# Two stacked transformer blocks on one core: when weights are split at the end of a projection, which engine computes three modulation vectors, and which one squares x in the opening

## The chip, the cores and the metric

The kernel runs on one core of a Trainium2 chip. The core has TensorE (PE; its weight loads are PEld), VectorE (DVE), ScalarE (ACT), GpSimd (POOL) and SyncE (SP, which here only issues transfers). Each engine works through its own instructions in the order in which they were written for it; semaphores make one wait for another. The metric is the device time of one execution in microseconds (us).

## The reference

Input `x` has 256 positions of 1024 numbers. Two blocks of two layers each follow each other. A layer is a mixer and a feed-forward part, each behind a modulated norm; the modulation comes from a condition vector `c`:

```python
def first_block(x, c, positions, ...):
    cond = jax.nn.silu(c)
    for l in range(DEPTH):                      # DEPTH = 2
        mod = cond @ w_mod[l] + b_mod[l]        # six vectors of 1024
        sh1, sc1, gt1, sh2, sc2, gt2 = [m[:, None, :] for m in jnp.split(mod, N_MOD, axis=-1)]
        h = rms_norm(x, norm_g[l, 0]) * (1.0 + sc1) + sh1
        y = mixer_block(h, positions, w_in[l], ...)   # conv, NSA, GLA, gMLP, then @ w_o
        x = x + gt1 * rms_norm(y, norm_g[l, 1])
        h = rms_norm(x, norm_g[l, 2]) * (1.0 + sc2) + sh2
        y = jnp.square(jax.nn.relu(h @ w_up[l])) @ w_down[l]
        x = x + gt2 * rms_norm(y, norm_g[l, 3])
    return x

def second_block(x, c, ...):
    c_act = jax.nn.silu(c)
    for l in range(DEPTH):
        mod = (c_act @ ada_w[l] + ada_b[l])[:, None, :]
        sh_m, sc_m, gt_m, sh_f, sc_f, gt_f = jnp.split(mod, 6, axis=-1)
        h = rms_norm_2(x, norm_mix[l]) * (1 + sc_m) + sh_m
        y = hybrid_mixer(h, ...) if l % 2 == 0 else retention_mixer(h, ...)
        x = x + gt_m * y
        h = rms_norm_2(x, norm_ffn[l]) * (1 + sc_f) + sh_f
        x = x + gt_f * swiglu(h, ffn_w_in[l], ffn_w_out[l])
    return x
```

All weights are float32, and the result is to be accurate as in float32.

## The kernel before, in words

**Data.** `x` stays on the chip, transposed: eight chunks of 128 features by 256 positions. A matrix is read in loads `w` of 1 MB (128 x 2048, pool of `W_BUFS` = 4), issued on SP in program order. `load_split` cuts a load into two halves of 128 x 1024 and each into a high part `wh` (a cast on ACT, L214) and the rest `wl` (a subtraction on DVE, L217). The activations are split alike: `hh` on ACT (L211), `hl` on DVE (L233), after `h` on DVE (L233). A product is then three matmuls (`hh` by `wh`, `hh` by `wl`, `hl` by `wh`) into PSUM tiles `pa`.

**Stages and tails.** The program runs layer by layer: input projection, mixer, output projection, feed-forward up, down. A *tail* is the end of a projection with the norm behind it. In block 1, `post1` sums squares of `y` (`sq`), of the gated tile `t`, and `xt` = t times x over the tiles; `px` matmuls with a matrix of ones sum them over the partitions; `rstd`, three `u` steps, `sx`, `r` follow, and then per chunk an update of `x`, `h`, `hh`, `hl`. In block 2, `post2` adds each tile to `x`, sums its squares, and `rstd` of that sum leads to `h` at once. There are seven tails: the first layer's output projection, three more in block 1, three in block 2 (behind the last projection there is none).

**The hold.** `sums` notes the last Square in `self.tail`. When `post1` or `post2` has read its last tile, it sets `self.tailed = 3`; the casts of the next three loads are then held until that Square has been issued on ACT:

```python
            with self.after(self.tail) if self.tailed else nullcontext():
                self.copy(h[:, :m], w[:, a * n:b * n])
```

`after` sets an order for the scheduler on an engine; where it holds nothing back, the scheduler places instructions by its own estimate of the times.

**Modulation.** `MODE` says how each of the six vectors of a layer is computed. "j": the first two of the first layer, in the opening (`mods_first`). "p": on TensorE (`mod`): eight transfers `mw` of 512 KB, for each four matmuls `pm`, then a copy `row` on ACT and four small transfers `ab<-row` by POOL. "d": on DVE (`mod_rows`): eight transfers, each multiplied by the condition's rows and summed in one instruction (L398, here called a product); `settle` keeps the last ones back until `last_wl`, the split issued last, has been written. The pool `mw` has four buffers. Modulation has a low priority (`LATER`). In the first layer `weave` gives out its steps between those of the mixer at the pace `FILL`; later ones are given out by `carry` at a rate per load.

**Opening.** Constants, angles and squares of the first `x` run in a written order on ACT, eight Squares there; sixteen `px` matmuls and the copy `sx` lead to `r`.

Of the kernel before, what the change touches and what calls it, by code (L numbers as in the profile page):

```python
# [12 lines left out]
AF = mybir.ActivationFunctionType  # L13
# [3 lines left out]
D = 1024  # L17
# [87 lines left out]
CONSTANTS_AT = 3  # L105
EARLY_AT = (0, 2)
AHEAD = 3
SQ_ACT = (0,)
# [3 lines left out]

MODE = {(1, 0): "jjpppd", (1, 1): "dddddd", (2, 0): "dddddd", (2, 1): "dddddd"}

# [8 lines left out]
LOADS = {"ffn10": (32, 3, 4), "ffn11": (32, 3, 4), "ffn20": (38, 3, 4), "ret": (32, 3, 4)}  # L123
FILL = (0.7, 0, 0)
W_BUFS, MW_BUFS, HL_BUFS = 4, 4, 4
# [9 lines left out]
class Prog:  # L135
    def __init__(self, ctx, tc, t):
# [17 lines left out]
        self.plan = None  # L154
        self.pend, self.hold, self.last_wl, self.tail, self.tailed = [], None, None, None, 0

# [160 lines left out]
    def load_split(self, ap, nk, n):  # L317

        w = self.load(ap, nk * n)
        self.tailed = max(self.tailed - 1, 0)  # L320
        parts = []
        hk = (nk + 1) // 2
        for a, b in ((0, hk), (hk, nk)):
            h = self.hlp.tile([128, 1024], F32R, name=self.nm("wh"), tag="wh")
            l = self.hlp.tile([128, 1024], F32R, name=self.nm("wl"), tag="wl")
            m = (b - a) * n
            with self.after(self.tail) if self.tailed else nullcontext():
                self.copy(h[:, :m], w[:, a * n:b * n])
# [56 lines left out]
    def silu_c(self, c):  # L385
        s = self.V(KD)
        self.sigmoid(s, c)
        self.mul(c, c, s)
        rep = self.C(KD, 32)
        self.copy(rep, c[:, :, None].to_broadcast([128, KD, 32]))  # L390
        return rep
# [47 lines left out]
    def mods_first(self, v):  # L439
# [7 lines left out]
        b1 = self.V(KD, s="b1")  # L447
        self.stt(b1, b[:, 8:16], 1.0, g[:, 0:8], ALU.add, ALU.mult)
        quad = self.C(1, s="quad")
# [50 lines left out]
    def sums(self, parts, src, keep=2):  # L500

        q = self.U(S, s="sq")
        self.tail = self.act(q, src, AF.Square)
        self.running(parts, q, keep)
# [21 lines left out]
    def norm_mod(self, r, scale, shift):  # L526

        hs, hm = [], []
        for c in range(4):
# [3 lines left out]
            for j in range(2):  # L533
# [3 lines left out]
                hm.append(self.stt(h[:, j], self.x[:, k], scale[:, k:k + 1], r, ALU.mult, ALU.mult))  # L537
                self.act(hi[:, j], h[:, j], AF.Identity, bias=shift[:, k:k + 1])
                self.last_lo = self.stt(lo[:, j], h[:, j], shift[:, k:k + 1], hi[:, j].bitcast(F32), ALU.add,
                                        ALU.subtract)  # L540
                hs.append((hi[:, j], lo[:, j]))
        self.update = None
        return hs

# [21 lines left out]
    def start(self):  # L566
# [14 lines left out]
        return c  # L581

    def constants(self):
        nc = self.nc
# [7 lines left out]
    def rope_tables(self):  # L592
# [17 lines left out]
        lim = 3.1415925  # L610
        self.ts(a, a, lim, ALU.min, -lim, ALU.max)
        self.act(self.rc, a, AF.Sin)
# [35 lines left out]
    def block1_vecs(self, l):  # L648
# [7 lines left out]
        return v  # L656

    def cond1(self):
        self.rows[1] = self.silu_rows(self.rows_c(self.t["c1"]))
        yield 1  # L660

# [456 lines left out]
    def post1(self, tiles, b, sx, **where):  # L1118
# [3 lines left out]
        for group in tiles:  # L1122
# [7 lines left out]
            for j, y in group:  # L1130
# [3 lines left out]
                self.running(xt, q, keep)  # L1134
        self.tailed = 3
        r = self.rstd(yy, D)
# [437 lines left out]
    def post2(self, tiles, gt, end=False):  # L1574
# [10 lines left out]
        if end:  # L1585
            return None
        self.tailed = 3
        return self.rstd(sq, D)
# [43 lines left out]
    def run(self):  # L1632
# [4 lines left out]
        with self.tc.manual_schedule(engines={mybir.EngineType.Activation}):  # L1637
            self.nc.scalar.preload_act_table_set("natural_log_exp_and_others")
            self.crep = {1: self.silu_c(c)}
            self.rope_tables()  # L1640
            self.nc.scalar.preload_act_table_set("natural_log_exp_and_others")
            sq = []
            for j in range(KD):
                self.sums(sq, self.x[:, j], KD)
            p = self.psum_of(sq)
            sx = self.U(S, s="sx")
            self.copy(sx, p)
            r = self.U(S, s="r2")
            self.rsqrt(r, sx, 1.0 / D)
        self.mods_first(self.v1[0])  # L1650
        for l in range(2):
            if l == 0:
                self.v1.append(self.block1_vecs(1))
                self.v1[1]["norm2"] = self.v1[1]["norm"][:, 16:24]
                self.queue = [self.cond1()] + [self.mods(*a, self.v1[0]) for a in STAGE["mix10"]]
            else:
                self.start2()
# [123 lines left out]
```

## Time and profile before

| what | value |
|---|---|
| three runs, median (lowest to highest) | 1537.33 us (1529.53 to 1538.15) |
| the profiled execution | 1532.73 us |
| its span | 1530.9 us |
| mean granted clock of TensorE | 0.973 |
| TensorE busy | 1445.3 us (94%) |
| VectorE busy | 1139.9 us (74%) |
| ScalarE busy | 808.4 us (53%) |
| moved by DMA | 333.15 MB, 218 GB/s |

Times in the rows are from the start of the span. The profiled execution took 1.8 us more than its span. "Busy" counts an engine's instructions; an idle engine off the chain costs nothing. A granted clock of 1.00 is 2.4 GHz, and half of it 1.2 GHz; a value between is a mean over a stretch.

### The profile page before, as it was taken

To read this page: it belongs to the slowest core of one execution; us is meant where nothing else is said; L and a number is where in the kernel's file an instruction comes from. 1 tells how busy PE (TensorE), PEld (TensorE's weight loads), DVE (VectorE), ACT (ScalarE), POOL (GpSimd) and SP (SyncE) were. 2 spreads that over 40 slices of the span, in tenths; PEclk is the share of its full clock that TensorE was granted. 3 is DMA by queue.
4 is the path that set the end of the run, shared out by engine and by line. 5 is a ranking of instruction groups with operands and counts; after the bars stand their busy time and mean duration, and the time that the engine had idled before them with its cause. 6 is when DMAs were issued, how large, how long until landed. Compare 5 with 4: busy or idle time off the path is not lost.

```text
span 1530.9 us, 28353 instructions
## 1 busy us (share of the span) xinstructions
PE 1445.3 (94%) x11594; PEld 1377.5 (90%) x11594; DVE 1139.9 (74%) x1966; ACT 808.4 (53%) x1348; POOL 19.4 (1%) x57
## 2 busy tenths in 40 slices
PE   7999799998999799998999988999989999899999
PEld 5986699997987799997998778999989999899999
DVE  4774779886786899987887547788678888577664
ACT  5654466544555555443774246565445555466642
POOL 1000100000000000000000000000000000000000
PEclk9999899999999999998999898999999999999999
DMA  9846679994441479983532016666766776445453
GB/s 367 289 189 233 234 258 349 358 336 167 140 188 56 168 286 356 375 316 132 220 113 109 1 56 234 243 233 234 267 246 244 259 257 240 163 157 189 167 168 107
DMA packets 65783, 333.15 MB, mean 218 GB/s; under 512 B 8146, under 2 KB 9460, under 8 KB 41716
## 3 DMA queue, kind: packets, MB, share of 16 engines
q1 hardware_dynamic: 65268, 331.30, 59.2%
q8 instruction: 91, 1.49, 0.4%
q14 instruction: 40, 0.33, 0.1%
q0 software_dynamic: 384, 0.03, 0.0%
HBM read 330.22 MB, written 1.05 MB: 216 GB/s over the span
## 4 chain that ended last, share of the span: by engine, by line
PE 91%; DVE 4%; ACT 2%; DMA 1%; issue 1%; SPq 0%; POOL 0%; DVEq 0%; ACTq 0%
PE pa L236 79%; PE py L236 5%; PE px L236 4%; DVE wl L217 2%; PE po L236 1%; PE pm L236 1%; ACT wh L214 1%; ACT u L211 0%; DMA ab<-row 0%; PE py L239 0%; DVE h L233 0%; DMA mw<-in_wmod 0%; DMA vec<-in_vec 0%; DVE u L217 0%; DVE t L217 0%
## 5 line engine op out<-in xcount | busy, mean ns | idle before, releaser
L217 DVE TENSOR_TENSOR wl<-w,wh 128x1024 fp32r<-128x1024 f32 (+4 forms) x444 | 512.5, 1161 | 214.6 <-ACT wh L214 213.5
L214 ACT CAST wh<-w 128x1024 fp32r<-128x1024 f32 (+4 forms) x444 | 439.9, 999 | 363.8 <-PE pa L236 338.6
L236 PE MATMUL pa<-hh,wh 128*128 128x256 f32 x1920 | 515.6, 289 | 43.9 <-ACT hh L211 43.9
L236 PE MATMUL pa<-hh,wl 128*128 128x256 f32 x1920 | 511.1, 287 | 0.0
L236 PEld LDWEIGHTS pa<-hh,wh 128*128 128x128 f32 x1920 | 373.0, 194 | 51.6 <-ACT hh L211 46.8
L236 PE MATMUL pa<-hl,wh 128*128 128x256 f32 x1920 | 390.1, 285 | 0.0
L236 PEld LDWEIGHTS pa<-hh,wl 128*128 128x128 f32 x1920 | 373.4, 195 | 2.3 <-issue 2.1
L236 PE MATMUL pa<-oh,wh 128*128 128x256 f32 x1184 | 334.4, 286 | 7.4 <-ACT oh L214 7.4
L236 PE MATMUL pa<-oh,wl 128*128 128x256 f32 x1184 | 332.6, 284 | 0.0
L236 PE MATMUL pa<-ol,wh 128*128 128x256 f32 x1184 | 318.6, 283 | 0.2
L236 PEld LDWEIGHTS pa<-hl,wh 128*128 128x128 f32 x1920 | 301.5, 193 | 1.9 <-issue 1.6
L236 PEld LDWEIGHTS pa<-oh,wh 128*128 128x128 f32 x1184 | 227.7, 192 | 12.3 <-ACT oh L214 9.1
L236 PEld LDWEIGHTS pa<-oh,wl 128*128 128x128 f32 x1184 | 226.9, 192 | 2.6 <-issue 1.3
L236 PEld LDWEIGHTS pa<-ol,wh 128*128 128x128 f32 x1184 | 219.2, 191 | 0.6 <-DVE ol L217 0.6
L398 DVE SCALAR_TENSOR_TENSOR mw<-mw,cond 128x1024 f32<-128x1024 f32 x152 | 182.8, 1219 | 0.0
L236 PE MATMUL pa<-wh,hh 128*128 128x256 f32 (+2 forms) x224 | 66.9, 301 | 6.2 <-ACT hh L211 6.2
L236 PE MATMUL pa<-wh,hl 128*128 128x256 f32 (+2 forms) x224 | 66.1, 302 | 1.2 <-DVE hl L233 1.2
L236 PE MATMUL pa<-wl,hh 128*128 128x256 f32 (+2 forms) x224 | 67.1, 300 | 0.0
L211 ACT ACTIVATE sw<-sw 128x256 f32<-128x256 f32 x132 | 55.0, 417 | 3.7 <-DVE sw L230 1.0
L211 ACT ACTIVATE u<-u 128x512 f32<-128x512 f32 (+3 forms) x78 | 42.6, 555 | 18.6 <-DVE u L230 13.1
L211 ACT ACTIVATE hh<-h,mods 128x256 fp32r<-128x256 f32 x64 | 30.7, 505 | 38.8 <-DVE h L233 33.6
L236 PEld LDWEIGHTS pa<-wh,hh 128*128 128x128 f32 x224 | 43.8, 196 | 7.7 <-ACT hh L211 6.6
(359 smaller groups left out, 1348.0 us busy)
## 6 DMA issues: line engine op xcount, KB each, us to landing
mw<-in_wmod SPq DMA_DIRECT2D x176, 512.0 KB, 5.7
w<-in_fwin SPq DMA_DIRECT2D x44, 1024.0 KB, 4.8
w<-in_wup SPq DMA_DIRECT2D x32, 1024.0 KB, 5.0
w<-in_wdn SPq DMA_DIRECT2D x32, 1024.0 KB, 6.7
w<-in_rwin SPq DMA_DIRECT2D x24, 1024.0 KB, 5.0
w<-in_fwo SPq DMA_DIRECT2D x32, 704.0 KB, 4.1
w<-in_win SPq DMA_DIRECT2D x16, 1024.0 KB, 6.1
w<-in_hwin SPq DMA_DIRECT2D x12, 1024.0 KB, 4.8
```

Of the source, the lines that this page charges most:

```text
L211: return self.nc.scalar.activation(out=out, in_=in_, func=func, **kw)
L214: return self.nc.scalar.copy(out, in_)
L217: return (e or self.nc.vector).tensor_tensor(out=out, in0=a, in1=b, op=op)
L236: return self.nc.tensor.matmul(out, lhsT=lhsT, rhs=rhs, start=start, stop=stop, skip_group_check=True)
L398: self.nc.vector.scalar_tensor_tensor(out=w, in0=w, scalar=1.0, in1=cond, op0=ALU.mult, op1=ALU.mult, accum_out=m[:, j:j + 1])
```

## The change

Three things change.

1. The hold on the casts of the three loads behind a tail goes. In its place the *second* `load_split` behind a norm has its casts after the `hh` of chunk 2 of that norm.
2. The first layer's vectors 3 to 5 (indices 2, 3 and 4) are computed as products on DVE ("d"), not by matmuls ("p"). Their pace `FILL` is 1.0, not 0.7. The condition's rows, which DVE needs for that, are loaded and computed in the opening instead of the mixer.
3. In the opening five of the eight squares of `x` go to DVE, 24 matmuls of ones by ones are added on TensorE ahead of the `px` sums, `r` is computed straight from PSUM and `sx` copied behind it, and the table load on ACT stands behind the Squares.

```diff
+X_ACT = (1, 3, 5)
+WARM = 24
-MODE = {(1, 0): "jjpppd", (1, 1): "dddddd", (2, 0): "dddddd", (2, 1): "dddddd"}
+MODE = {(1, 0): "jjdddd", (1, 1): "dddddd", (2, 0): "dddddd", (2, 1): "dddddd"}
-FILL = (0.7, 0, 0)
+FILL = (1.0, 0, 0)
...
     def load_split(self, ap, nk, n):
         w = self.load(ap, nk * n)
-        self.tailed = max(self.tailed - 1, 0)
+        self.since += 1
...
-            with self.after(self.tail) if self.tailed else nullcontext():
+            with self.after(self.hold_act) if self.since == 2 and self.loads > 2 else nullcontext():
                 self.copy(h[:, :m], w[:, a * n:b * n])
...
-        self.stt(b1, b[:, 8:16], 1.0, g[:, 0:8], ALU.add, ALU.mult)
+        with self.after(self.angles):
+            self.stt(b1, b[:, 8:16], 1.0, g[:, 0:8], ALU.add, ALU.mult)
...
-        self.tail = self.act(q, src, AF.Square)
+        self.act(q, src, AF.Square)
...
-                self.act(hi[:, j], h[:, j], AF.Identity, bias=shift[:, k:k + 1])
+                hh = self.act(hi[:, j], h[:, j], AF.Identity, bias=shift[:, k:k + 1])
+                if k == 2:
+                    self.hold_act = hh
...
         self.update = None
+        self.since = 0
         return hs
...
+    def warm(self):
+
+        ps = self.M(128)
+        for i in range(WARM):
+            self.mm(ps, self.ones, self.ones, i == 0, i == WARM - 1)
...
-    def cond1(self):
-        self.rows[1] = self.silu_rows(self.rows_c(self.t["c1"]))
-        yield 1
...
-        self.tailed = 3
         r = self.rstd(yy, D)
...
-        self.tailed = 3
         return self.rstd(sq, D)
...
             self.rope_tables()
-            self.nc.scalar.preload_act_table_set("natural_log_exp_and_others")
             sq = []
             for j in range(KD):
-                self.sums(sq, self.x[:, j], KD)
+                if j in X_ACT:
+                    self.sums(sq, self.x[:, j], KD)
+                else:
+                    q = self.U(S, s="sq")
+                    with self.after(self.angles), self.after(self.silu):
+                        self.mul(q, self.x[:, j], self.x[:, j])
+                    self.running(sq, q, KD)
+            self.nc.scalar.preload_act_table_set("natural_log_exp_and_others")
+            self.warm()
             p = self.psum_of(sq)
+            r = self.U(S, s="r2")
+            self.rsqrt(r, p, 1.0 / D)
             sx = self.U(S, s="sx")
             self.copy(sx, p)
-            r = self.U(S, s="r2")
-            self.rsqrt(r, sx, 1.0 / D)
         self.mods_first(self.v1[0])
+        with self.later(LATER):
+            self.rows[1] = self.silu_rows(self.rows_c(self.t["c1"]))
...
-                self.queue = [self.cond1()] + [self.mods(*a, self.v1[0]) for a in STAGE["mix10"]]
+                self.queue = [self.mods(*a, self.v1[0]) for a in STAGE["mix10"]]
```

What the scheduler makes of it is seen at three places. The first is ACT at the last tail, from the retention's output projection to the second SwiGLU. Before (`sq` of the last tile, casts of the first two loads, `rstd`, `hh` of the norm):

```order
L211 ACTIVATE sq_15076<-x_88 128x256
L214 CAST wh_15124<-w_15122 128x1024
L214 CAST wh_15128<-w_15122 128x1024
L214 CAST wh_15189<-w_15187 128x1024
L214 CAST wh_15193<-w_15187 128x1024
L211 ACTIVATE rstd_15082<-px_15079,eps_90 128x256
L211 ACTIVATE rstd_15082<-rstd_15082 128x256
L211 ACTIVATE hh_15086<-h_15085,mods_11419 128x256 x2
L211 ACTIVATE hh_15095<-h_15094,mods_11419 128x256 x2
```

The same place with the change:

```order
L216 CAST wh_15101<-w_15099 128x1024
L216 CAST wh_15105<-w_15099 128x1024
L213 ACTIVATE sq_14990<-x_88 128x256
L213 ACTIVATE sq_15053<-x_88 128x256
L213 ACTIVATE rstd_15059<-px_15056,eps_90 128x256
L213 ACTIVATE rstd_15059<-rstd_15059 128x256
L213 ACTIVATE hh_15063<-h_15062,mods_11396 128x256 x2
L213 ACTIVATE hh_15072<-h_15071,mods_11396 128x256
L216 CAST wh_15166<-w_15164 128x1024
L216 CAST wh_15170<-w_15164 128x1024
L213 ACTIVATE hh_15072<-h_15071,mods_11396 128x256
```

The first load's two casts moved ahead of the last two Squares, and the second load's between the third and the fourth `hh`.

The second place is DVE at the first tail, behind the first layer's output projection. Before (`xt` of the last tile, splits of the first two loads of the feed-forward part, the `u` steps):

```order
L217 TENSOR_TENSOR xt_1940<-t_1933,x_88 128x256
L217 TENSOR_TENSOR xt_1946<-t_1935,x_88 128x256
L217 TENSOR_TENSOR wl_2113<-w_2110,wh_2112 128x1024
L217 TENSOR_TENSOR wl_2117<-w_2110,wh_2116 128x1024
L217 TENSOR_TENSOR wl_2183<-w_2180,wh_2182 128x1024
L217 TENSOR_TENSOR wl_2187<-w_2180,wh_2186 128x1024
L217 TENSOR_TENSOR u_1964<-rstd_1953,px_1956 128x256
L233 SCALAR_TENSOR_TENSOR u_1964<-px_1960,u_1964 128x256
L217 TENSOR_TENSOR u_1964<-u_1964,rstd_1953 128x256
L217 TENSOR_TENSOR sx_1968<-u_1964,sx_148 128x256
```

The same place with the change (`mw` by `cond` is a product):

```order
L400 SCALAR_TENSOR_TENSOR mw_2015,mod_2006<-mw_2015,cond_433 128x1024
L219 TENSOR_TENSOR u_1976<-rstd_1965,px_1968 128x256
L400 SCALAR_TENSOR_TENSOR mw_2018,mod_2006<-mw_2018,cond_433 128x1024
L235 SCALAR_TENSOR_TENSOR u_1976<-px_1972,u_1976 128x256
L400 SCALAR_TENSOR_TENSOR mw_2021,mod_2006<-mw_2021,cond_433 128x1024
L219 TENSOR_TENSOR u_1976<-u_1976,rstd_1965 128x256
L400 SCALAR_TENSOR_TENSOR mw_2024,mod_2006<-mw_2024,cond_433 128x1024
L219 TENSOR_TENSOR sx_1980<-u_1976,sx_176 128x256
```

The splits left this place, and products stand between the steps of the tail.

The third place is SP's queue at the same tail, from the end of the first layer's output projection (`in_wo`) to the feed-forward part (`in_wup`). Before:

```order
L277 DMA w_1868<-in_wo 128x2048
L277 DMA w_2110<-in_wup 128x2048
L482 DMA mw_1616<-in_wmod 128x1024
L482 DMA mw_1620<-in_wmod 128x1024
L482 DMA mw_1974<-in_wmod 128x1024
L482 DMA mw_1978<-in_wmod 128x1024
L277 DMA w_2180<-in_wup 128x2048
```

With the change:

```order
L279 DMA w_1880<-in_wo 128x2048
L408 DMA mw_1988<-in_wmod 128x1024
L408 DMA mw_1991<-in_wmod 128x1024
L279 DMA w_2087<-in_wup 128x2048
L279 DMA w_2157<-in_wup 128x2048
L279 DMA w_2223<-in_wup 128x2048
L279 DMA w_2293<-in_wup 128x2048
L408 DMA mw_1994<-in_wmod 128x1024
L408 DMA mw_1997<-in_wmod 128x1024
L408 DMA mw_2000<-in_wmod 128x1024
```

Four loads of the next stage now stand in a row ahead of most of the vectors' transfers, which wait behind them.

## Rows read from the trace of the kernel before

**Rows 1.** The chain that ended last, by line, from the page.
```profile
PE pa L236 79%; PE py L236 5%; PE px L236 4%; DVE wl L217 2%; PE po L236 1%; PE pm L236 1%; ACT wh L214 1%; ACT u L211 0%; DMA ab<-row 0%; PE py L239 0%; DVE h L233 0%; DMA mw<-in_wmod 0%; DMA vec<-in_vec 0%; DVE u L217 0%; DVE t L217 0%
```

**Rows 2.** Windows of the seven idle stretches of TensorE, their sum.
```profile
sum 48.60, PE 0.10 PEld 0.03 DVE 44.70 ACT 25.36 POOL 3.16; mean PE 0.01 PEld 0.00 DVE 6.39 ACT 3.62 POOL 0.45
```

**Rows 3.** Timeline of ACT at the last tail: start, duration, instruction.
```profile
1330.83 3.87 ACT L214 CAST wh<-w 128x1024 fp32r<-128x1024 f32 x4
1334.60 0.46 ACT L211 ACTIVATE rstd<-px,eps 128x256 f32<-128x256 f32 x1
...
1336.95 0.91 ACT L211 ACTIVATE hh<-h,mods 128x256 fp32r<-128x256 f32 x2 [1.44 <-DVE h L233]
```

**Rows 4.** Timeline of DVE there.
```profile
1331.89 4.63 DVE L217 TENSOR_TENSOR wl<-w,wh 128x1024 fp32r<-128x1024 f32 x4 [1.48 <-ACT wh L214]
```

**Rows 5.** Timeline of TensorE there, the last sum.
```profile
1330.97 0.70 PE L236 MATMUL px<-sq,ones 128*128 128x256 f32 x2 [0.66 <-ACT sq L211]
```

**Rows 6.** Timelines of DVE, second `u` step, block 1's last three tails.
```profile
379.69 0.42 DVE L233 SCALAR_TENSOR_TENSOR u<-px,u 128x256 f32<-128x256 f32 x1
...
518.36 0.42 DVE L233 SCALAR_TENSOR_TENSOR u<-px,u 128x256 f32<-128x256 f32 x1
...
713.03 0.42 DVE L233 SCALAR_TENSOR_TENSOR u<-px,u 128x256 f32<-128x256 f32 x1
```

**Rows 7.** Timelines of TensorE, last `px`, the same three tails.
```profile
374.24 1.03 PE L236 MATMUL px<-xt,ones 128*128 128x256 f32 x4
...
513.03 1.46 PE L236 MATMUL px<-xt,ones 128*128 128x256 f32 x6
...
710.10 1.03 PE L236 MATMUL px<-xt,ones 128*128 128x256 f32 x4
```

**Rows 8.** Windows after idle stretches; clock, DMA share, GB/s last.
```profile
758.60:768.00 9.40, 7.76 (x61) 7.28 (x62) 8.82 (x18) 9.24 (x19) 0.00 (x0) 1.00 0.31 113
888.30:898.00 9.70, 6.36 (x31) 6.35 (x31) 2.90 (x7) 4.04 (x7) 0.00 (x0) 0.65 0.00 0
1337.50:1343.90 6.40, 6.39 (x38) 6.39 (x39) 5.63 (x14) 3.11 (x8) 0.00 (x0) 0.68 0.55 227
```

**Rows 9.** The chain in order of time, first layer: start, duration, what.
```profile
139.51 5.25 DMA mw<-in_wmod
...
154.69 0.98 PE pm L236 x4
...
161.73 1.85 PE pm L236 x14
163.58 5.84 PE pa L236 x47
...
178.55 5.99 DMA ab<-row
...
185.06 0.52 ACT hh L211
```

**Rows 10.** Windows of mixer layer 0, mixer layer 1, output projection layer 0.
```profile
42.00:145.80 103.80, 102.12 (x767) 81.14 (x767) 72.54 (x156) 57.22 (x120) 2.33 (x6) 1.00 0.64 233
392.90:488.50 95.60, 92.09 (x727) 81.13 (x725) 71.06 (x151) 54.32 (x118) 0.22 (x3) 1.00 0.42 149
145.80:169.40 23.60, 23.60 (x189) 21.05 (x188) 12.79 (x28) 10.32 (x23) 2.05 (x4) 1.00 0.65 241
```

**Rows 11.** Timeline of DVE, two products of later vectors in a row.
```profile
208.39 1.22 DVE L398 SCALAR_TENSOR_TENSOR mw<-mw,cond 128x1024 f32<-128x1024 f32 x1
...
209.53 1.22 DVE L398 SCALAR_TENSOR_TENSOR mw<-mw,cond 128x1024 f32<-128x1024 f32 x1
```

**Rows 12.** Timeline of DVE, last split of layer 0's output projection.
```profile
157.54 1.22 DVE L217 TENSOR_TENSOR wl<-w,wh 128x1024 fp32r<-128x1024 f32 x1
```

**Rows 13.** Opening: ACT's squares, and the window at 35 us.
```profile
10.18 2.56 ACT L211 ACTIVATE sq<-x 128x256 f32<-128x256 f32 x8
...
35.00:40.00 5.00, 5.00 (x74) 4.14 (x65) 1.74 (x4) 2.94 (x7) 0.00 (x0) 1.00 1.03 418
```

More of the change, by code (lines that the diff above doesn't have):

```diff
@@ L154, in __init__ @@
         self.plan = None
-        self.pend, self.hold, self.last_wl, self.tail, self.tailed = [], None, None, None, 0
+        self.pend, self.hold, self.last_wl = [], None, None
     def nm(self, s):
@@ L387, in silu_c @@
         self.sigmoid(s, c)
-        self.mul(c, c, s)
+        self.silu = self.mul(c, c, s)
         rep = self.C(KD, 32)
@@ L610, in rope_tables @@
         lim = 3.1415925
-        self.ts(a, a, lim, ALU.min, -lim, ALU.max)
+        self.angles = self.ts(a, a, lim, ALU.min, -lim, ALU.max)
         self.act(self.rc, a, AF.Sin)
```

## The prediction

> **What bounds the kernel now.** I first read the chain that ended last: TensorE carries it nearly alone, with `pa` matmuls at 79%, `py`, `px`, `po` and `pm` behind, and small remainders for DVE splits `wl`, ACT casts `wh` and the transfers `ab<-row` and `mw<-in_wmod` [rows 1]. A kernel whose chain is TensorE gains only from work taken off TensorE or from TensorE's idle time, so the second view is the windows around its idle stretches. Seven of them are the tails: the last tile of an output projection, then a norm, then the first matmul of the next projection. Together they hold 48.6 us without a matmul [rows 2]. What fills one is seen at the last (retention to SwiGLU): right after the last Square, ACT runs four casts, 3.87 us, and only then the two activations of `rstd` [rows 3]; DVE runs four splits, 4.63 us, until 1336.52 [rows 4], and only then `h`; yet the sum that `rstd` needs left TensorE at 1331.67 [rows 5]. So the tail waits for splits that serve the stage after it. The third view is the first layer's tail and mixer, the only place where modulation vectors go through `pm` [rows 9, 10].
>
> **Hold dropped, block 2 (three tails).** The first load's casts and splits move ahead of the last Squares, where ACT and DVE have slack; the second load's come among the norm's `hh` and `h`. What ends last is then `px`. From its end, 1331.67, I count 0.05 to start, 0.46 and about 0.45 for the two activations and 0.5 for the first `h`: `hh` at about 1333.3 in place of 1336.95 [rows 3, 5]. That is 3.65 per tail; the idle stretch falls from 5.8 (0.5 for `hh`, then the first matmul at 1337.5) to about 2.15. Three such tails: **−10.95**.
>
> **Hold dropped, block 1 (the three tails after the first).** Here `rstd`, `u`, `sx`, `r` and an update of `x` follow each other. The second `u` step needs the last `px`; it began at 379.69, 518.36 and 713.03 [rows 6], while `px` ended at 375.27, 514.49 and 711.13 [rows 7]. With about 0.05 between, it could start 4.4, 3.8 and 1.85 earlier (the last of the three splits 520 columns, not 1024), and all behind it moves along: **−10.05**. Idle time is left there, some 4.4 us each.
>
> **What is given back.** The second load's two casts (1.94, half of the 3.87) and two splits (2.3, half of the 4.63) now lie between the norm's steps, where DVE was busy for 5.63 of 6.40 us at the last tail [rows 8]. DVE has 0.8 us there, so that up to 1.5 us a tail can reach TensorE if it wants tiles as fast as they come, and 2.3 at the worst; nothing, if TensorE is still slow. It is slow: the granted clock in that window was 0.68, a mixture of 1.2 and 2.4 GHz, worth 2.0 us of 6.4 [rows 8]. Which way this goes hangs on the clock. After an idle stretch of 1.67 us at 758.6 it stayed at 1.00; after one of 3.34 us at 888.3 it was 0.65 over the window [rows 8]. The three block 2 tails, at 2.15 us, stand nearer to the first, so they may keep 2.4 GHz: they win up to 2.0 us and lose up to 1.5 to 2.3 us for splits that come too late. I take 0 for them (each −2 to +2.3). The three of block 1 keep over 4 us of idle time, so the clock still falls and hides most of the splits; between 0 and 2.3 each I take 0.9, **+2.7**.
>
> The Trainium skill (TensorE: Matmul & The Clock Gate, "HAM oscillation") says that idle stretches between bursts of matmuls bring the clock back to its lower level, and that the gap's length decides. The rows agree in kind: 1.67 us at full clock, 3.34 us not. By that rule alone, block 2's tails would come out at up to 6 us better together than I take them; no row here has a gap of 2.15 us.
>
> **First layer's vectors 3 to 5 on VectorE.** It removes 24 groups of four `pm` matmuls, three row copies and twelve transfers `ab<-row`, and with them the last transfer's 5.99 us, on which `hh` waited at 185.06 [rows 9]. It adds 24 products: their starts are 1.14 us apart [rows 11]. Eight fall in the mixer, sixteen behind the last split of the output projection.
> Mixer: 103.8 us with vectors, against 95.6 us for the same stage in layer 1 with none (DVE 71 of 95.6, so a quarter idle) [rows 10]. Removed are `pm` and a 5.25 us wait of `pm` for its transfer [rows 9]. Eight products cost DVE 9.2 us; between 0 (all in its idle time) and 9.2 I take 1.5, since three quarters of DVE's idle time would be enough. So the mixer takes about 97.1: −6.7. The output projection took 23.6 without an idle moment [rows 10], of it 0.98 and 1.85 in `pm` [rows 9]: 20.8 after.
> First tail: this is where I expect most of it to be lost. Before, the last split of the output projection ended at 158.76 [rows 12], 10.6 before the projection's end at 169.4, or 8.7 without the `pm` that came in between. With the opening's −1 (below), TensorE would finish at 41 + 97.1 + 20.8 = 158.9 and that split at 150.2. Behind it DVE has 16 products × 1.14 = 18.3, two splits of the first load 2.3, and some 23 small steps of the tail (sums, `xt`, `u`, `x`), each about 0.35 apart by the 0.42 of a `u` step [rows 6], 8.1: 28.7. The first of them wait some 2 us for transfers, for the queue has the four loads of the next stage ahead of them. `hh` comes at 150.2 + 30.7 + 0.2 = **181.1** against 185.06: **−4.0**, though TensorE finished 10.5 us earlier. Bounds: if the products were all hidden, `hh` would follow TensorE's end by some 8 us as the other block 1 tails do, at 167; if the rounds of four buffers wait for transfers (512 KB at the 418 GB/s of the opening [rows 13] is 1.25 us, a round some 6.5 us), at 187. The rows on both sides are far apart; the products' own sum is the nearer, so I keep it.
>
> The Trainium skill (Vector Engine (DVE) Microarchitecture Reference, "Points that are easy to get wrong") says that a scalar-tensor-tensor step with two sources in SBUF that are not bf16 halves throughput. That would make a product some 2.1 us, an estimate, and the tail some 15 us longer. The rows decide against it: the same product is 1.22 us long and follows the next at 1.14.
>
> **Opening.** Five of eight squares leave ACT: eight took 2.56 [rows 13], so 1.6 us less there; five go to DVE, idle at that time. 24 warming matmuls come in TensorE's idle time. Against it, the condition's rows (512 KB) now load ahead of the last vector loads, at 418 GB/s and a DMA share of 1.03 [rows 13], 1.25 us. The opening is bounded by its transfers and by TensorE's matmuls, both full in the window at 35 us [rows 13], so I take **−1** (−3 to +2); it is in the 181.1 above.
>
> **Sum.** −10.95 − 10.05 + 2.7 − 4.0 = −22.3 from the profiled execution's 1532.7 (span 1530.9 and 1.8 around it): 1510.4. The median of the three runs is 4.6 above that execution, so I put the forecast a third of that way up: **1512**.
>
> **Rivals.**
> A. The first tail costs more: the rounds of four buffers bind, `hh` at 187 to 190, 6 to 9 us worse: **1520**. For it: sixteen products behind one engine that also does the norm. Against it: DVE, not the queue, adds up to the longer sum.
> B. The tails' gain comes back in the stage behind each: the second load's splits stall TensorE by 1.5 to 2.3 in all six, 9 to 14 in place of 2.7: **1523**. For it: DVE 5.63 of 6.40. Against: the lower clock there.
> C. The products do not bind in the first tail; `hh` near 169: **1500**. For it: TensorE's idle stretch hides transfers; against: the 28.7 of DVE work.
> D. Slower. The second load's casts wait behind `hh`, so that its splits are exposed whole: 4.2 us in each of six stages, 25 in all; and in block 2's three, where the gap alone would not have done it, this new stall brings the clock down, as at 888.3, where 0.65 over 9.7 us means 3.4 lost [rows 8]: 10 more. Against 35 stand the 21 of the tails and the 4 of the first layer, so 10 above the time before: **1543**. It decides from 4.2 us lost in each stage (25 over six). Against it: TensorE has the first load's 48 matmuls to do in the meantime, at 0.124 us each [rows 9] 6 us.
> E. The change does not do what it says: the casts are not ahead of the last Squares in time because their loads have not landed. Then `px` still ends when it does, and half of the 21 us goes; near B in time (1523), and counted with it.
> F. Block 2's tails, at 2.15 us of idle time, keep 2.4 GHz as after the 1.67 us at 758.6 [rows 8], and the splits come in time all the same: 2.0 less at each of three, 6 in all: **1506**. For it: the nearer of the two rows; against: at full clock TensorE wants the second load's splits sooner.
> The Trainium skill's page above (TensorE: Matmul & The Clock Gate, "HAM oscillation") is that rule carried through.
>
> **How the numbers follow.** Forecast 0.50, A 0.14, B with E 0.13, C 0.10, F 0.10, D 0.03. A measurement tells about 1% from no change, 15 us: faster by more means below 1522. The forecast with its own spread (1506 to 1520), C, F and most of A lie below, with a part of B: 0.74. Within 1%: the rest of A and B and the forecast's upper edge, 0.23. Slower 0.03. The range leaves out D and the lower half of C and the tops of A and B: 1498 to 1526.
>
> **What would show it.** In block 2's tails: `rstd` right behind the last `px`, no cast between it and the last Square, idle stretches near 2.2 us, and the granted clock behind them near 1.00 or at 0.7. In block 1's: 4.4 us. In the first layer: no `pm`, a mixer near 97 us, a tail of some 22 us in which products follow each other on DVE. I am wrong if the tails' idle time moves into the stage behind (B, D), if the products leave DVE waiting for transfers (A), or if the mixer takes more than 100 us.

## The result and the profile after

The changed kernel takes 1515.98 us (median of four runs, 1514.56 to 1519.28) against 1536.54 us for the kernel before, run beside it: a ratio of 0.9878, 95% interval 0.9843 to 0.9913. The profiled execution took 1515.14 us, its span is 1513.3 us, 17.6 us less than before.

A ledger from the two ACT timelines, by the first `hh` behind each tail, shows where the time went (us). The first column runs from the start of the span to the first `hh` behind the first tail, the last from the last tail's first `hh` to the end of the span. Each column holds the stages up to a tail and that tail.

| | first tail | to 2nd | to 3rd | to 4th | to 5th (hybrid) | to 6th | to 7th | to the end |
|---|---|---|---|---|---|---|---|---|
| before | 185.06 | 198.41 | 138.67 | 194.67 | 205.37 | 200.40 | 214.37 | 193.95 |
| after | 180.86 | 194.51 | 136.02 | 194.76 | 207.29 | 195.57 | 210.75 | 193.54 |
| difference | -4.20 | -3.90 | -2.65 | +0.09 | +1.92 | -4.83 | -3.62 | -0.41 |

The chain by line, from the page of the changed kernel. `pm` is nearly gone from it (0%, against the 1% of [rows 1]); what is left under that name are the warming matmuls of the opening. What VectorE's products `mw` have on it, 1%, is new:

```profile
PE pa L238 77%; PE px L238 5%; PE py L238 4%; PE po L238 1%; DVE wl L219 1%; DVE h L235 1%; DVE mw L400 1%; ACT wh L216 1%; DVE t L219 1%; ACT u L213 1%; DVE x L219 1%; PE pm L238 0%; DVE hl L235 0%; ACT hh L213 0%; ACT rstd L213 0%
```

The windows of the changed kernel (stretch, length, busy time of PE, PEld, DVE, ACT, POOL, then clock, DMA share, GB/s). The first two are the first layer's mixer and output projection, which answer to [rows 10]. Then come TensorE's idle stretches at the first four tails and the last one, and the 6.4 us behind the fifth, sixth and seventh tail, which answer to [rows 8]:

```profile
44.90:137.70 92.80, 89.62 (x694) 78.60 (x694) 76.59 (x165) 52.53 (x114) 0.14 (x2) 0.98 0.60 224
137.70:158.30 20.60, 20.56 (x168) 20.27 (x168) 17.31 (x32) 12.36 (x25) 0.00 (x0) 1.00 0.46 158
172.30:181.40 9.10, 0.00 (x0) 0.00 (x0) 9.07 (x22) 1.46 (x4) 0.00 (x0) 0.68 0.88 307
371.50:375.90 4.40, 0.04 (x1) 0.00 (x0) 4.25 (x12) 1.43 (x3) 2.85 (x8) 0.74 0.01 2
507.60:511.90 4.30, 0.00 (x0) 0.00 (x0) 4.23 (x12) 1.44 (x3) 0.00 (x0) 0.79 0.08 31
702.30:706.70 4.40, 0.02 (x1) 0.00 (x0) 4.27 (x12) 1.43 (x3) 0.00 (x0) 0.77 0.19 60
1318.20:1320.30 2.10, 0.04 (x1) 0.00 (x0) 0.89 (x3) 1.44 (x4) 0.00 (x0) 1.00 0.00 0
914.00:920.40 6.40, 5.47 (x41) 5.06 (x42) 6.40 (x13) 4.02 (x8) 0.00 (x0) 1.00 0.06 10
1109.60:1116.00 6.40, 6.27 (x38) 5.94 (x39) 6.40 (x13) 4.01 (x8) 0.00 (x0) 0.73 0.24 77
1320.30:1326.70 6.40, 5.45 (x41) 5.04 (x42) 6.40 (x13) 4.02 (x8) 0.00 (x0) 1.00 0.02 5
```

The idle stretch of block 2's tails is 2.1 us where 2.15 was forecast. The three of block 1 that follow the first are 4.4, where some 4.4 was forecast. The mixer is 92.8 us and the output projection 20.6; 97.1 and 20.8 were forecast. (The mixer's windows do not begin at the same point: the last `hh` of the opening begins at 42.12 before and at 44.30 after. From there the mixer is 103.7 us before and 93.4 after.) In the windows behind block 2's tails the clock is 1.00, 0.73 and 1.00, and yet at 1.00 TensorE is busy for only 5.47 and 5.45 of 6.40 us: it waits. For what, the timeline of ACT at the last tail shows, which answers to [rows 3]:

```profile
1317.07 0.42 ACT L213 ACTIVATE sq<-x 128x256 f32<-128x256 f32 x1 [4.82 <-DVE x L235]
1318.28 0.47 ACT L213 ACTIVATE rstd<-px,eps 128x256 f32<-128x256 f32 x1 [0.79 <-PE px L238]
...
1319.76 0.91 ACT L213 ACTIVATE hh<-h,mods 128x256 fp32r<-128x256 f32 x2 [0.55 <-DVE h L235]
1321.21 0.51 ACT L213 ACTIVATE hh<-h,mods 128x256 fp32r<-128x256 f32 x1 [0.55 <-DVE h L235]
1321.63 1.98 ACT L216 CAST wh<-w 128x1024 fp32r<-128x1024 f32 x2
1323.52 1.30 ACT L213 ACTIVATE hh<-h,mods 128x256 fp32r<-128x256 f32 x3
```

`rstd` follows the last Square by 0.8 us with no cast between, and `hh` comes 1.5 us after `px` ended (1318.24) instead of 5.3. But the third `hh` is followed by the second load's two casts, 1.98 us, and the fourth `hh` stands behind them at 1323.52: TensorE stands still from 1323.35 to 1324.07, and for 0.21 us up to 1322.03, where it waits for an `hl`. These two are what it is idle in that window.

The kernel before held the casts of two loads there, not of three: `load_split` takes one off `tailed` before it asks for it, and the four casts of [rows 3] are those of two loads.

The chain in order of time at the first tail of the changed kernel, which answers to [rows 9]. Where `ab<-row` stood, products and tail steps now alternate on VectorE, up to the first `h`:

```profile
150.80 3.24 DVE mw L400 x5
154.24 1.23 DVE mw L400 x3
...
166.84 5.47 PE px L238 x12
...
172.76 1.14 DVE mw L400 x2
174.24 1.14 DVE mw L400 x2
...
176.72 1.15 DVE mw L400 x2
...
180.02 0.40 DVE h L235
```

### The profile page after: what moved, and what is told of

It reads as the page before. It is cut to its first block, busy times and chain, and to the rows that moved or that the text cites. A ratio compares the mean times of both kernels' runs of the same rounds, so it can differ in the third digit from the quotient of the medians.

```text
span 1513.3 us, 28210 instructions
## 1 busy us (share of the span) xinstructions
PE 1434.2 (95%) x11546; PEld 1377.6 (91%) x11546; DVE 1166.1 (77%) x2016; ACT 805.7 (53%) x1340; POOL 13.0 (1%) x45
## 4 chain that ended last, share of the span: by engine, by line
PE 89%; DVE 6%; ACT 3%; issue 1%; POOL 0%; ACTq 0%; DVEq 0%
PE pa L238 77%; PE px L238 5%; PE py L238 4%; PE po L238 1%; DVE wl L219 1%; DVE h L235 1%; DVE mw L400 1%; ACT wh L216 1%; DVE t L219 1%; ACT u L213 1%; DVE x L219 1%; PE pm L238 0%; DVE hl L235 0%; ACT hh L213 0%; ACT rstd L213 0%
## 5 line engine op out<-in xcount | busy, mean ns | idle before, releaser
L400 DVE SCALAR_TENSOR_TENSOR mw<-mw,cond 128x1024 f32<-128x1024 f32 x176 | 212.2, 1219 | 0.0
L213 ACT ACTIVATE hh<-h,mods 128x256 fp32r<-128x256 f32 x64 | 31.2, 506 | 35.3 <-DVE h L235 30.9
L213 ACT ACTIVATE u<-u 128x512 f32<-128x512 f32 (+3 forms) x78 | 42.8, 557 | 13.3 <-DVE u L232 11.3
```

What stands on the lines that cost most here:

```text
L213: return self.nc.scalar.activation(out=out, in_=in_, func=func, **kw)
L400: self.nc.vector.scalar_tensor_tensor(out=w, in0=w, scalar=1.0, in1=cond, op0=ALU.mult, op1=ALU.mult, accum_out=m[:, j:j + 1])
```

## The experiments

All times are medians in us; the ratio is to the kernel before, run beside each (its medians were 1534.96 to 1536.15). Where two runs had different medians of the kernel before beside them, the text below compares what each gained on its own.

| run | what it is | median (range) | ratio (95%) | first `hh` of the first tail | hybrid column |
|---|---|---|---|---|---|
| e1_tails | tails alone | 1516.52 (1514.85 to 1517.98) | 0.9879 (0.9859 to 0.9899) | 183.25 | 205.64 |
| e2_vectors | vectors alone | 1536.83 (1532.63 to 1537.68) | 1.0013 (1.0002 to 1.0024) | 189.98 | 207.07 |
| e3_opening | opening alone | 1538.31 (1535.58 to 1542.29) | 1.0025 (1.0013 to 1.0037) | 188.35 | 207.04 |
| e4_no_second_hold | changed, no new hold | 1516.14 (1515.46 to 1518.16) | 0.9880 (0.9863 to 0.9897) | 181.82 | 208.28 |
| e5_tails_vectors | tails and vectors | 1512.14 (1511.17 to 1513.11) | 0.9842 (0.9828 to 0.9855) | 180.75 | 202.59 |
| e6_tails_opening | tails and opening | 1521.11 (1518.73 to 1522.17) | 0.9898 (0.9884 to 0.9911) | 185.61 | 206.06 |
| e7_cond_in_mixer | changed, condition's rows in the mixer | 1515.70 (1514.21 to 1519.63) | 0.9868 (0.9854 to 0.9883) | 180.94 | 207.11 |
| e8_one_on_pe | changed, one vector on TensorE | 1519.04 (1517.31 to 1520.05) | 0.9885 (0.9872 to 0.9899) | 182.98 | 207.27 |
| e9_block2_tails | hold off block 2's tails alone | 1523.52 (1521.54 to 1524.54) | 0.9922 (0.9909 to 0.9934) | 183.75 | 206.58 |
| e10_pace2 | e5 with pace 2.0 | 1518.85 (1515.34 to 1519.56) | 0.9887 (0.9872 to 0.9902) | 185.14 | 203.34 |
| e11_no_second_hold_old_opening | e5 without the new hold | 1519.07 (1516.95 to 1523.64) | 0.9897 (0.9881 to 0.9913) | 186.35 | 207.65 |
| e12_short_products | changed, products over 64 columns | 1508.75 (1507.44 to 1514.55) | 0.9834 (0.9809 to 0.9859) | 174.43 | 207.10 |

**The three parts alone.** e1 is the kernel before with the edits of the hold, as in the diff above. e2 is the kernel before with

```diff
-MODE = {(1, 0): "jjpppd", ...
+MODE = {(1, 0): "jjdddd", ...
-FILL = (0.7, 0, 0)
+FILL = (1.0, 0, 0)
```

and e3 the kernel before with the edits of `run`, `warm`, `b1`, `X_ACT` and `WARM`, the condition's rows left where they were.

> The kernel before with the first part alone: no hold on the casts behind a tail, the second load's casts behind the third hh. Theory (the tails' waits were real and are given back only in part): the six tails behind the first give 21 us at the first hh, 3 to 4 come back in the stages behind them, the first tail gives nothing since it waits for ab; and the hybrid mixer, whose order on VectorE comes out nearly as in the changed kernel, loses the 4.5 us that it lost there: 13 to 14 us faster than before, 0.991. Rival (the hybrid's loss comes from another part of the change): 18 us faster, 0.988. Rival (the gain is absorbed behind each tail): under 8 us, 0.995 or more.

> The kernel before with the second part alone: vectors 3 to 5 of the first layer on VectorE at pace 1.0, the condition's rows still loaded in the mixer. Theory (TensorE ends the output projection some 11 us earlier without pm, and the first tail gives most of it back, since 16 products follow one another on VectorE there): 4 to 7 us faster, first hh of the first tail at 178 to 181 us. Rival (the products stall the mixer's own VectorE work too): 0 to 4 us slower. Rival (hidden): 12 us faster or more.

> The kernel before with the third part alone, but for the condition's rows, which stay in the mixer: squares on two engines, 24 warming matmuls, r straight from PSUM. Theory (the first hh comes 5 us earlier, but the opening's end is bound by the transfers of the first two vectors; the 2.9 us that the changed kernel lost at the opening's end come from the condition's rows): 0 to 2 us faster, last hh of the opening at 41 to 42 us. Rival (the loss comes from the squares and the new order itself): last hh at 44 us, 2 to 3 us slower.

The tails alone give 18.6 us (1535.1 to 1516.5), most of the 20.6 of the whole change. The vectors alone cost 1.7, the opening alone 3.2. Their sum is 13.7 faster; measured together they are 20.6 faster. So the parts interact by some 7 us, with an interval of 5 us either way on the whole change alone.

e1's clean theory held for the six tails (its columns fall by 4.4, 1.9, 0, ..., 4.8, 3.3), but its median is the rival's, 18 us. The rival's reason did not hold: e1's hybrid column is 0.3 us longer than before although its tail is 3.7 shorter, so the hybrid mixer lost some 4 us in e1 too. What the theory had missed is the first tail: it also gained, 1.8 us at the first `hh`. Before, the four casts stood ahead of the activations of `rstd` and of `row` there too. With that, theory and spans agree (15.5 us); the rest of the 18.6 is that the profiled execution of the kernel before, 1532.73, was faster than its median.

e2's total is its first rival's (0 to 4 us slower), but not for the reason given: TensorE's last `px` ended at 171.11, where it ended at 177.60 before. The time went behind it. The first `hh` comes at 189.98, 18.9 us after that `px`. The chain of e2 there shows the old hold and the products together, with splits, products and a transfer one behind the other:

```profile
168.90 1.87 DVE wl L217 x2
171.09 1.24 DVE mw L398 x2
172.35 7.37 DMA mw<-in_wmod
...
186.18 1.14 DVE mw L398 x2
...
188.05 1.14 DVE mw L398 x2
...
189.98 0.52 ACT hh L211
```

e3's last `hh` of the opening began at 42.33 (42.12 before), near what its theory said, while its median is nearer the rival's. What the opening costs is taken up behind the pairs.

**The parts in pairs.** e5 is before with e1's and e2's edits; e6 before with e1's and e3's; e7 the changed kernel with

```diff
-            self.rows[1] = self.silu_rows(self.rows_c(self.t["c1"]))
...
-                self.queue = [self.mods(*a, self.v1[0]) for a in STAGE["mix10"]]
+                self.queue = [self.cond1()] + [self.mods(*a, self.v1[0]) for a in STAGE["mix10"]]
```

> The kernel before with the first two parts, tails and vectors, the condition's rows in the mixer and the old opening. Alone the tails measured 1516.5 and the vectors 1536.8 against 1535.1. Theory (the parts interact: with the old hold the first tail had four splits and 16 products on VectorE behind TensorE's end, 18.9 us to the first hh; without the hold the splits lie earlier and only the products bind, and the earlier end of TensorE is kept in part): 1511 to 1513, first hh of the first tail 177 to 179. Rival (the parts add): 1518, first hh at 187 or later.

> The kernel before with the first and the third part, tails and opening, the vectors on TensorE as before. Theory (the opening costs what it cost alone, 3.2 us, whatever stands behind it): 1519 to 1521. Rival (the opening's loss alone was the granted clock of two short stretches and is not there in this company): 1515 to 1517.

> The changed kernel, but the condition's rows are loaded and computed in the mixer's queue as before, not in the opening. Theory (moving them into the opening took 512 KB and three activations ahead of the last vectors, some 2 us of the opening, and freed the mixer of the same work, so that little is left): within 2 us of the changed kernel, 1514 to 1518. Rival (they are dear in the opening): 1511 to 1513.

e5 came out at 1512.14, within the theory of interaction and far from the 1518 of a sum: with the hold gone, the vectors give 5.4 us (e1 gained 18.6 on the kernel before, e5 24.0) in place of costing 1.7, and 5.5 in the other pair (e6 15.0, the changed kernel 20.6). At the first `hh` that is 4.75 us between e6 and the changed kernel. Between e1 and e5 it is 2.5, which may be all the opening of e1's profiled execution (its last `hh` began at 44.89, e5's at 42.22, with the same code); 3.05 more lie in the hybrid column. e5's first `hh` came later than expected (180.75, not 177 to 179). e6 shows the opening's cost again, 3.6 us against the tails alone, but e5 and e7, which differ by the opening, have the same first `hh` (180.75 and 180.94): behind the products the opening's cost cannot be seen. What separates e5 from e7, 3.6 us, lies in the hybrid column, 202.59 against 207.11. e7 equals the changed kernel: where the condition's rows are loaded does not matter.

e6's rival named the clock, and the traces bear on it. The changed kernel and e4 have the same 515 matmuls in the same order in their first 60 us, and up to 18.5 us TensorE is busy for the same time in both, to 0.01 us in each of four stretches. Then the clock falls in the one (first line) and not in the other (e4, second line):

```profile
18.50:25.40 6.90, 6.41 (x54) 5.49 (x58) 2.84 (x3) 2.32 (x3) 0.00 (x0) 0.51 1.02 390
18.50:25.40 6.90, 6.03 (x94) 4.55 (x94) 2.85 (x3) 3.11 (x6) 0.00 (x0) 1.00 1.05 394
```

The 150th `pa` matmul begins at 58.92 in the changed kernel, at 56.21 in e4, and at 55.95 before. So the new opening at full clock loses next to nothing, and gains nothing either. A stretch at 1.2 GHz lies in the first 50 us of six of the seven traces with the new opening, and of two of the seven with the old one (e1 and e2, whose 150th is 2.8 us later than before). The opening's cost of some 3 us may well be this; with one trace of each kernel, it is not shown that the new opening brings it on.

**The new hold.** e4 is the changed kernel, e11 is e5, both with

```diff
-            with self.after(self.hold_act) if self.since == 2 and self.loads > 2 else nullcontext():
+            with nullcontext():
```

> The changed kernel without the new hold on the second load's casts: the scheduler then puts them ahead of the last Square too. Theory (what was given back behind the tails came from these casts and splits among the norm's steps): the three tails of block 1 win back about 1.4 us each and those of block 2 about 1, and the last Square is not late, since ACT has slack there: 5 to 7 us faster than the changed kernel, about 1509. Rival (the casts, now ahead of the last Square, delay it by up to 2 us at each tail): 6 to 12 us slower than the changed kernel, 1522 to 1528.

> Tails and vectors with the old opening (1512.1), without the new hold on the second load's casts. Its order in the hybrid mixer is nearly that of the changed kernel, the slower one. Theory (the second hold costs 1 to 2 us at each tail of block 1; the hybrid's order costs 4.5): 48 matmuls after each tail of block 1 done 1.4 to 2 us earlier, the hybrid stage 206 to 208 us, 1511 to 1514 in all. Rival (the order is not what costs in the hybrid): 1506 to 1509.

In e4 the 144th `pa` matmul after the first `hh` began at 23.8, 19.3 and 22.9 us behind block 1's second to fourth tail, against 25.6, 21.1 and 24.1 in the changed kernel: 1.8, 1.8 and 1.2 us won back, as the theory had it, and the last Squares were not late. ACT's timeline at the second tail of e4 has the steps of the norm at their plain distance, with no cast between them:

```profile
375.49 0.51 ACT L213 ACTIVATE hh<-h,mods 128x256 fp32r<-128x256 f32 x1 [1.45 <-DVE h L235]
376.22 0.51 ACT L213 ACTIVATE hh<-h,mods 128x256 fp32r<-128x256 f32 x1 [0.22 <-DVE h L235]
377.68 0.51 ACT L213 ACTIVATE hh<-h,mods 128x256 fp32r<-128x256 f32 x1 [0.95 <-DVE h L235]
379.14 0.51 ACT L213 ACTIVATE hh<-h,mods 128x256 fp32r<-128x256 f32 x1 [0.95 <-DVE h L235]
```

But the total is the changed kernel's (1516.14). The first tail is 1.0 us later, the hybrid column 1.0, and the last two columns together 2.6 us longer. e11 came out well above both theories (1519.07): its tails won as in e4 (144th `pa` matmul at 23.8, 19.1, 22.9), and it lost 5.6 us at the first tail and 5.1 in the hybrid against e5. So the hold costs what was said behind the tails, and dropping it pays nothing here: the scheduler's order in the hybrid mixer changes with it (e4 and e11 have one order there, and it is not the changed kernel's). Where e11's 5.6 us at the first tail come from was not followed.

**What binds the first tail.** e8, e10 and e12:

```diff
-MODE = {(1, 0): "jjdddd", ...          # e8
+MODE = {(1, 0): "jjddpd", ...
-FILL = (1.0, 0, 0)                     # e10
+FILL = (2.0, 0, 0)
-            self.nc.vector.scalar_tensor_tensor(out=w, in0=w, scalar=1.0, in1=cond, ...
+            self.nc.vector.scalar_tensor_tensor(out=w[:, :n], in0=w[:, :n], scalar=1.0, in1=cond[:, :n], ...
```

> The changed kernel with one of the three vectors (index 4) back on TensorE, so that 16 products instead of 24 are left on VectorE, 8 behind the last split. Theory (the first tail is bound by the products on VectorE): the first hh comes 5 to 8 us earlier, 173 to 176, less 2 for the pm matmuls: 1509 to 1512. Rival (the row copy and its four transfers end last instead, 6 us behind the last pm): the first hh at 181 or later, no gain.

> Tails and vectors with the old opening (1512.1), and the pace of the vectors in the mixer at 2.0 in place of 1.0: 15 of the 24 products lie ahead of the last split of the output projection, not 8. Theory (the first tail is bound by the products behind that split, and the mixer has VectorE time to spare): first hh 4 to 8 us earlier, 173 to 177, 1504 to 1508. Rival (each product in the mixer costs it what the tail wins): first hh at 180 to 182, 1511 to 1514.

> The changed kernel, with the 24 products of the first layer's vectors 3 to 5 over 64 of their 1024 columns (the other columns are left out of those sums; all transfers stay). Theory (VectorE's products bind the first tail): the products take a tenth of their time, the first hh comes some 10 us earlier, at 169 to 173, and most of that reaches the end: 1505 to 1509. Rival (the transfers of these vectors bind, behind four loads in SP's queue and in a pool of four buffers): first hh at 177 to 181 with VectorE idle before each product, 1513 to 1516.

e12's first `hh` lies between its theory and its rival, and its median within the theory. With products 0.15 us apart the first `hh` comes at 174.43, 6.4 us earlier than in the changed kernel, so VectorE's products were a bound. But `px` ended at 161.15, and the 13.3 us from there are now transfers, in rounds of four buffers, as e12's chain shows:

```profile
152.21 8.21 DMA mw<-in_wmod
160.44 0.24 DVE mw L400 x2
160.71 7.27 DMA mw<-in_wmod
168.00 0.24 DVE mw L400 x2
168.26 5.61 DMA mw<-in_wmod
...
174.43 0.52 ACT hh L213
```

Both are there: the products end last in the changed kernel by 6.4 us, and right under them lie the transfers of 512 KB behind the four loads. More buffers for `mw` were not tried. e8 and e10 make the tail short (3.8 us from the last `px` to `hh` in both), and lose more than that ahead of it: TensorE's last `px` ends at 179.16 in e8, in place of 172.29 in the changed kernel, and at 181.32 in e10, in place of 171.16 in e5. The output projection starts at 145.4 in e8, with the `pm` matmuls back in the mixer, and at 141.2 in e10, with 15 products in it; the changed kernel and e5 start it at 137.7. So e8's first `hh` is its rival's, but not for the rival's reason (no `ab<-row` is on the chain there), and e10 is later and slower than both its forecasts. With seven products more in the mixer, four of them lie on e10's chain between 99.7 and 108.9 us, and a stretch of 6.8 us at 1.2 GHz follows, which e5 does not have. So VectorE's idle time there is not free for them; how the 3.5 us divide between products and clock is not shown.

**The hybrid mixer.** e9 is the kernel before without `self.tailed = 3` in `post2`.

> The kernel before with the hold taken off only the three tails of block 2 (nothing in its place); block 1 keeps it. The hybrid mixer's order on ACT and VectorE then comes out as in the kernel before but for a few rows at its end. Theory (the hybrid mixer loses 4 to 5 us in the changed kernel because the scheduler, with another time at its start, writes another order there): hybrid stage at its old speed, 201 to 202 us from first hh to first hh, the three tails 11 us shorter, 1524 to 1526. Rival (the loss is in the timing of loads or the clock, not in the order): 204 to 207 us for that stage, 1528 to 1530.

The total is 0.5 us below its theory; the three tails came out as forecast. The hybrid column is the rival's, 206.58. But the theory on the order can be read off another way: e9's TensorE has the same sequence of matmuls there as the kernel before, and up to 138 us behind the first `hh` the two agree to 0.4 us. Then e9 falls back by 5.7 us within 9 us, and stays behind. There its clock is 0.50 for 23.9 us, in the kernel before for 10.2 (the timelines give 843.24 to 853.48):

```profile
712.74:851.00 138.26, 132.77 (x958) 122.79 (x959) 108.22 (x242) 85.63 (x150) 1.05 (x2) 0.93 0.36 133
839.50:863.40 23.90, 23.07 (x85) 18.95 (x85) 9.25 (x27) 4.28 (x8) 0.62 (x2) 0.50 0.00 0
```

In the changed kernel the loss is earlier and goes with an order: 66 us into the stage ACT has the activations of `u` from `px`, two casts and three `cs` steps ahead of the next `u` from `cs`, and `px` waits for that one. In the kernel before, the `u` from `cs` comes first. At the 500th matmul of the stage, 69.6 us into it before, the changed kernel is 8.7 us behind, 1.2 of which it brought from the tail. Its chain there:

```profile
773.08 1.03 ACT wh L216
774.11 0.53 ACT u L213
774.64 0.53 ACT cs L213
...
775.83 1.00 ACT wh L216
...
776.85 1.23 DVE wl L219
...
779.40 2.61 PE px L238 x6
```

e6, e7 and e8, whose ACT order in this mixer is the changed kernel's row for row, have 206.06 to 207.27; e5 and e10, with another, have 202.59 and 203.34. All of these have a tail behind the mixer that is 3.7 us shorter than before. The changed kernel and e8, whose order there is the same on every engine, agree to 0.1 us over the whole stage.

But e5 and e10 are not free of the loss. At the 500th matmul e5 is 6.1 us behind the kernel before, 2.1 of it from the tail, and e10 6.2 and 1.2; of all the runs only e9 does not fall back there. e5 makes it up later: from the 900th matmul to the 1000th it wins 5.3 us on the kernel before and the changed kernel 2.6, neither of them at 1.2 GHz, where the kernel before has its 10.2 us. So two things are shown: times that go with the order (same order, same times until the clock parts them; e5's order 3.4 us better than the changed kernel's up to the 500th matmul, and 2.7 more behind the 900th), and the clock (5.7 us in e9). Why a given edit leads the scheduler to the slower order is open, and it wasn't tried to fix the order by hand.

## Why the prediction was right, point by point

- **Tails, block 2** (forecast -3.65 each): measured -3.73, -3.76, -3.76 from `px` to `hh`. Right (the four pieces counted there add up to 1333.13, not 1333.3, a slip of 0.2 us). In e9, with the hold off these three alone, they measure the same; that its median fell by 11.4 us, as they would have it, is luck in part, since its trace has 4.9 us more in the hybrid mixer and 4.1 us less ahead of it.
- **Tails, block 1** (-4.4, -3.8, -1.85): the time from the last `px` to the first `hh` fell by 4.38, 3.83 and 1.86. Right. That the second `u` step begins when the last `px` ends was the whole working.
- **Given back** (+2.7 in block 1, 0 in block 2): by the 144th `pa` matmul after the first `hh`, +1.0, +1.95 and +1.2, together 4.2, and -1.1, +0.4 and -0.3 in block 2. Right in kind; block 1's term was too small by 1.5. e4 shows that it is the second load's casts and splits.
- **Rival F**, at 0.10, was half there. The clock stayed at 1.00 in two of the three tails, but that won 1.1 us at one and 0.3 at the other, not 2.0 each: at full clock TensorE waits for the fourth `hh` instead. The 48th matmul comes 7.78 and 7.73 us behind the first `hh` with no fall of the clock, and 8.17 with one. The Trainium skill (TensorE: Matmul & The Clock Gate, "HAM oscillation"), by which the length of a gap decides on the clock, agrees only in part here: over the changed kernel and ten of the runs above, the same gap of 2.07 us led to a stretch at 1.2 GHz in 28 of 33 cases, and to none in 5. In the changed kernel two `px` matmuls, 0.70 us, behind another idle 0.59, stand ahead of that gap at the last tail.
- **First layer** (-4.0 at the first `hh`): measured -4.2, but made of other pieces. From the last `hh` of the opening, the mixer gained 10.3, not 6.7; the output projection 3.0, not 2.8; the opening lost 2.2 in place of winning 1 (its last `hh` moved from 42.12 to 44.30, although the first came 5.3 earlier), and e4, where it begins at 43.13 at full clock, puts about half of that to the clock. The term of 1.5 for eight products in the mixer did not show; they need 9.2 of its 24.5 us of idle DVE time, not the three quarters of the working. The tail came out as said: 30.0 us from the end of the last split (150.89) to `hh`, where 30.9 were summed from 150.2. e12 shows the sum's two halves, the products and the transfers under them, to be both near the end. That the whole came out at -4.2 is luck in part: the opening's miss and the mixer's cancel.
- **The term that failed by its sign** is the split of the sum by parts: the prediction gave the first layer's 4 us to the vectors. Alone they cost 1.7; they give 5 us only with the hold gone, which the prediction didn't say. And the opening's -1 was +3.2 alone.
- **What the sum lacked**: the hybrid mixer's +4.5 (beyond what was given back behind its tail), an order that came with the edit. It is the size of the miss: the sum came to -22.3 in the profiled execution, the span fell by 17.6.
- **A better version**: e5, tails and vectors without the opening's edits, at 1512.14 (1511.17 to 1513.11), below e7, the changed kernel's equal, at 1514.21 to 1519.63 beside it. As far as the traces show, that is its hybrid stage, and not its opening.

## What to carry to other kernels

A tail that waits for preparatory work of the next stage can be costed from two rows: when the sum that the norm needs has ended, and when the preparatory work has; their distance came back to about 0.1 us at all six places. Costs of parts that share one engine at one place (splits and products on VectorE at the first tail) don't add, so such parts are to be tried in pairs before one is judged by itself. With a scheduler that orders by its own estimates, an edit can draw a new order in stages that it doesn't touch; some four us of this kernel's difference went with that, and only a comparison of stages, not of totals, shows it. And a stage is to be read with its clock: one trace of a kernel can lose 3 us to it in an opening that another kernel with the same matmuls runs at full clock.

## What the hardware did that was not expected

The same sequence of matmuls ran equal to 0.4 us for 138 us and then parted by 5.7 us, when in one run a stretch at 1.2 GHz lasted 23.9 us, with TensorE busy for 23.07 of it by the rows, and in the other 10.2. In the opening, two traces with the same matmuls and the same busy times up to 18.5 us had a granted clock of 0.51 and of 1.00 in the 6.9 us behind. And the same idle stretch of 2.07 us was followed by a fall of the clock in 28 of 33 cases and by none in five.
